# A hybrid two-layer trunk on one core: softmax sums divide a head's result, queries negated, operands moved by pads, residual squares added on VectorE

## The chip, the cores and the metric

The kernel runs on 1 core of one Trainium2 chip. The metric is the device time of one execution in microseconds (us). TensorE is written PE, its weight loads PEld, VectorE DVE, ScalarE ACT, GpSimd POOL, and SyncE, which issues the DMAs, SP.

## The reference, cut to what matters

Two layers work on 256 tokens of 1024 features. In each, a token mixer (layer 0: a state-space mixer called S5; layer 1: causal attention with 12 heads of 64 and a linear bias by distance, ALiBi) runs beside a 4-head attention into 256 memory tokens; both are concatenated and go through one output projection, and a SwiGLU FFN follows. With 256 tokens the block-sparse attention is one block, so layer 1 is plain causal attention.

```python
scores = jnp.einsum('bshd,bmhd->bhsm', qh, mem_k)        # qh is scaled by 64 ** -0.5
p = jax.nn.softmax(scores, axis=-1)
out = jnp.einsum('bhsm,bmhd->bshd', p, mem_v)
...
s_own = jnp.where(dist_own >= 0, s_own - slopes * dist_own, NEG_INF)
p = softmax(s_own);  out = p @ v_own
...
x = x + jnp.concatenate([tok, mem_out], axis=-1) @ w_out[i]
h = _rmsnorm(x, ffn_norm_g[i])
x = x + (jax.nn.silu(h @ w_gate[i]) * (h @ w_up[i])) @ w_down[i]
```

## The kernel before, in words

**Layout.** Activations lie transposed: features on the 128 partitions, the 256 tokens along the row. Every fp32 operand of the large products is split into a high and a low part in the format fp32r (`split`, `split_hi`, `split_lo`), and `mm3` makes one product of three matmuls: high by high, high by low, low by high. In a matmul one operand is loaded into PE and stays (PEld shows the load), the other streams by.

**Weights** come in chunks of 128x1024 by DMA into `raw`; ACT or POOL writes `whi`, DVE or POOL writes `wlo` (`split_hi`, `split_lo`; L140, L158). `rings` opens the three pools, `plan` sets the order of the chunks and the engines for each.

**Stages.** S5 mixer with four memory heads (`mixers0`), `w_out`, gate and up products (`ffn`), the down product, then for layer 1 attention with 4 memory heads and 12 causal ones (`mixers1`), which ends with its own output projection, gate and up again, and last `finale`, where the down product takes the tokens as output partitions and the weights as the streaming operand.

**Order.** `ORDER0` and `ORDER1` are lists of step names; each is emitted in that order, and the framework's scheduler may move instructions of different steps past each other on an engine. Each engine then works strictly in its own order. For head i the steps are `s` (scores), `x` (maximum and exponential), `n` (division by the sum), `t` (transposition of the weights p on PE), `h` (split of the transposed p into `ph` and `pl`), `p` (product with the values, bank `pv`) and `o` (result into the concatenated activations, `gl` or `mcat`). There is one PSUM bank of kind `pv`, and two of kind `tp`.

**Heads in pairs.** Two heads of 64 make one 128-row tile. In `h_values` the values (high part in columns 0 to 63, low part in 64 to 127) are the loaded operand, and the weights p stream by, 256 columns for a memory head's halves and 256 and 128 for a causal head's; so the result stands with head features on the partitions, the low part's result in partitions 64 to 127. `h_out` adds the two halves.

**Residuals.** `residual` adds a product to x on DVE, writes the next norm's input (`scaled`: high part on ACT, low part on DVE) and squares x on ACT; `square` then adds the squares of tiles 1 to 6 on POOL (L199). This is done 8 times after each of `w_out`, the first down product and layer 1's output projection.

Of the kernel before, what the change touches and what calls it, by code (L numbers as in the profile page):

```python
# [17 lines left out]
P = 128  # L18
D = 1024
KT = D // P  # L20
T = 256
# [10 lines left out]
MAGIC = 12582912.0  # L32
SLOPES = [float(np.float32(2.0 ** (-8.0 * (n + 1) / HEADS))) for n in range(HEADS)]
# [30 lines left out]
tm4 turn2 xh0 rot3 wo5 sh1 nh0 xh1 wp4 rot4 scan3 th0 turn3 nh1 y2 st4 hh0 sh2 sh3 rot5 ab5 y3 ph0 th1 xh2 wp5 scan4  # L64
turn4 st5 scan5 gelu1 tm5 hh1 turn5 y4 nh2 y5 th2 xh3 gelu2 gA ph1 nh3 oh0 th3 gB hh2 oh1 gC0 ph2 oh2 gC1 hh3 ph3
oh3 gC2 gC3
# [8 lines left out]
q0 rc a4 v0a v0b rr q1 mq0 mq1 s0 s1 x0 kp0 n0 x1 ve0 a5 t0 n1 h0 s2 x2 a6 qp0 t1 s3 x3 h1 p0 qe0 n2 kp1 ke0  # L75
o0 n3 p1 a7 t2 h2 s4 x4 qp2 p2 s5 t3 h3 o1 qp1 a8 n4 qe1 t4 ke1 p3 kp2 x5 s6 s7 x6 h4 qp3 p4 qe2 n5 o2 a9 t5
v1a ke2 qe3 x7 n6 v1b h5 ve1 p5 t6 s8 x8 n7 s9 o3 t7 a10 kp3 a11 x9 h6 h7 o4 p6 n8 t8 qp4 o5 o6 qe4 n9 a12 h8
ke3 a13 p7 s10 s11 x10 v2a p8 o7 t9 o8 h9 n10 a14 x11 kp4 p9 t10 h10 n11 v2b p10 o9 ke4 t11 h11 ve2 s12 s13
kp5 p11 x12 qp5 x13 n12 n13 qe5 o10 o11 t12 ke5 a15 s14 x14 s15 t13 x15 h12 p12 n14 o12 w0 h13 p13 t14 n15 t15
h14 h15 p14 o13 o14 w1 p15 o15 w2 r0 r1 r2 w3 w4 w5 w6 w7 r3 r4 r5 r6 r7  # L80
# [6 lines left out]
class Trunk:  # L87
# [9 lines left out]
    def rings(self, ctx, nm, raw, hi, lo, ahead):  # L97
# [3 lines left out]
        self.n_raw = raw  # L101

# [84 lines left out]
    def square(self, sums, x, k):  # L187

        nc = self.nc
        if k == 0:  # L190
            sums.append(self.tmp.tile([P, T], F32, tag="acc", name="acc"))
            nc.scalar.activation(out=sums[0], in_=x, func=AF.Square)
            return
        s = self.tmp.tile([P, T], F32, tag="sq", name="sq")
        nc.scalar.activation(out=s, in_=x, func=AF.Square)  # L195
        if k == KT - 1:
            sums.append(s)
        else:
            nc.gpsimd.tensor_add(out=sums[0], in0=sums[0], in1=s)  # L199
# [103 lines left out]

    class Head:
        pass

    def mem_heads(self, out):
        hs = []
        for pr in range(2):
            for e in range(2):  # L310
                h = self.Head()
                h.slope, h.q, h.k, h.e = None, self.mq[pr], self.mk[pr], e
                h.vt, h.hd, h.out = self.mv, 2 * pr + e, out[pr]
                hs.append(h)
        return hs

    def moba_heads(self, p, q, k, vt, out):
        hs = []
        for e in range(2):
            h = self.Head()  # L320
            h.slope, h.q, h.k, h.e = SLOPES[2 * p + e], q, k, e
            h.vt, h.hd, h.out = vt, (2 * p + e) % 4, out
            hs.append(h)
        return hs

    def h_scores(self, h):
# [5 lines left out]
        if h.slope is None:  # L332
            h.blocks = [(0, slice(0, T)), (1, slice(T, 2 * T))]
            h.order, h.n0 = [0, 2, 1, 3], 0
# [3 lines left out]
        else:  # L338
            h.blocks = [(0, slice(0, P)), (1, slice(P, P + T))]
            h.order, h.n0 = [0, 1, 2], P  # L340
# [3 lines left out]
    def h_exp(self, h):  # L344
        nc, v = self.nc, self.nc.vector
        nm = self.small.tile([P, 2], F32, tag="nm", name="nm")
        if h.slope is None:
            src = h.s
            v.tensor_reduce(nm, src.rearrange("p (a b) -> p a b", a=2), axis=AX.X, op=ALU.max, negate=True)
# [7 lines left out]
        h.sm = self.small.tile([P, 2], F32, tag="sm", name="sm")  # L357
        h.p = self.tmp.tile([P, 512], F32, tag="p", name="p")
        for i, c in h.blocks:
            nc.scalar.activation(out=h.p[:, c], in_=src[:, c], func=AF.Exp, bias=nm[:, i:i + 1],  # L360
                                 accum_out=h.sm[:, i:i + 1])

    def h_norm(self, h):
        nc, v = self.nc, self.nc.vector
        ri = self.small.tile([P, 2], F32, tag="ri", name="ri")
        v.reciprocal(ri, h.sm)
        for i, c in h.blocks:
            v.tensor_scalar_mul(h.p[:, c], h.p[:, c], ri[:, i:i + 1])  # L368

    def h_turn(self, h):  # L370
        h.tp = self.bank("tp")
        for i, c in enumerate(h.order):
            self.nc.tensor.transpose(h.tp[:, i * P:(i + 1) * P], h.p[:, c * P:(c + 1) * P], self.ident)

    def h_split(self, h):
        n = len(h.order) * P
# [5 lines left out]
    def h_values(self, h):  # L382
        mm = self.nc.tensor.matmul
        n = len(h.order) * P
        o = h.o = self.bank("pv")
# [6 lines left out]
    def h_out(self, h):  # L392
        nc, v = self.nc, self.nc.vector
        r = slice(64 * h.e, 64 * h.e + 64)
        if h.e == 0:
            self.ot = self.tmp.tile([P, T], F32, tag="otile", name="otile")
        t = self.tmp.tile([P, T], F32, tag="ot", name="ot")
        nc.scalar.activation(out=t[r], in_=h.o[64:128, 0:T], func=AF.Copy)
        v.tensor_add(out=self.ot[r], in0=h.o[0:64, 0:T], in1=t[r])  # L399
        if h.e == 1:  # L400
            self.split(*h.out, self.ot)

    def head_blocks(self, do, nm, at):

        for k, f in (("s", self.h_scores), ("x", self.h_exp), ("n", self.h_norm),
# [495 lines left out]
    def mixers1(self, pool, xs, sums, cat, order):  # L901
# [43 lines left out]
        def alibi(i):  # L945

            sb = pool.tile([P, 384], F32, tag="sb", name="sb", bufs=3)
            self.nc.gpsimd.tensor_scalar(sb, self.dist, -SLOPES[i - MEMH], 1.0, op0=ALU.mult, op1=ALU.mult)
# [201 lines left out]
    def run(self):  # L1150
# [176 lines left out]
```

## Time and profile before

| | |
|---|---|
| three runs | 651.79, 659.34 and 661.03 us, median 659.34 |
| profiled execution, its own time | 652.99 us |
| its span, first to last instruction | 651.2 us |
| PE, PEld busy | 619.1, 589.0 us |
| DVE, ACT, POOL busy | 461.0, 363.8, 112.3 us |
| granted PE clock, mean | 0.981 |

The profiled execution lies with the fastest of the three runs; 1.8 us of its time lie outside the span. PE's records overlap, since matmuls are pipelined: how fast it works is read from the distance between the starts of matmuls, not from their durations. The stages of the profiled execution, by the weights and tiles that its rows name: S5 mixer with memory heads to 137 us, `w_out` to 161, gate and up to 280, down to 345, attention to 440 (its projection's first chunks among it), the rest of the projection to 460, gate and up to 581, `finale` to the end.

### The profile page before, as it was taken

What the parts mean: (1) busy time and instruction counts of PE and PEld (TensorE: products, weight loads), DVE (VectorE), ACT (ScalarE), POOL (GpSimd) and SP (SyncE); (2) the same over time, 40 slices, a digit from 0 to 9 for tenths busy, and PEclk for the clock granted to TensorE, in tenths of its full rate; (3) what the DMA queues carried; (4) which work ended last, traced back from release to release, by engine and by line L of the source; (5) the groups of instructions that cost most, each with busy time, mean ns of one, the idle gap of its engine ahead of it and who ended that gap; (6) DMA issues with size and microseconds to landing.
All of it is one profiled execution on the core that took longest, in us unless ns stands there. A gap on an engine that the chain in (4) does not pass through costs nothing. (4 is left out here: it accounts for less than half of the span.)

```text
span 651.2 us, 12337 instructions
## 1 busy us (share of the span) xinstructions
PE 619.1 (95%) x4808; PEld 589.0 (90%) x4808; DVE 461.0 (71%) x835; ACT 363.8 (56%) x651; POOL 112.3 (17%) x94
## 2 busy tenths in 40 slices
PE   7998889899999999999999999989999999999995
PEld 6887678799999999999999899979899999998884
DVE  7979778779766666655546989968676666664444
ACT  7494836667555555544444767747455555553333
POOL 2435531212000000001147522215000000000001
PEclk9999989999999999999999999989799999999998
DMA  7463231636555555555545234326455555554511
GB/s 222 166 192 113 66 98 57 201 131 224 183 193 195 194 196 195 178 180 183 192 174 202 103 129 136 126 98 192 148 180 194 194 195 194 196 195 164 192 64 66
DMA packets 35578, 105.82 MB, mean 162 GB/s; under 512 B 4032, under 2 KB 9280, under 8 KB 35520
## 3 DMA queue, kind: packets, MB, share of 16 engines
q1 hardware_dynamic: 35520, 105.03, 48.0%
q8 instruction: 38, 0.62, 0.4%
q14 instruction: 20, 0.16, 0.1%
HBM read 102.40 MB, written 1.05 MB: 159 GB/s over the span
## 5 line engine op out<-in xcount | busy, mean ns | idle before, releaser
L140 ACT ACTIVATE whi<-raw 128x1024 fp32r<-128x1024 f32 (+2 forms) x176 | 183.3, 1043 | 156.9 <-PE mm L183 108.2
L158 DVE TENSOR_TENSOR wlo<-raw,whi 128x1024 fp32r<-128x1024 f32 (+1 forms) x157 | 191.2, 1219 | 54.3 <-PE mm L1108 28.3
L1046 DVE TENSOR_TENSOR gu<-mm,rr 128x512 f32<-128x512 f32 x44 | 30.4, 692 | 51.3 <-PE mm L184 50.7
L158 POOL TENSOR_TENSOR wlo<-raw,whi 128x1024 fp32r<-128x1024 f32 (+2 forms) x19 | 44.6, 2355 | 45.4 <-issue 13.8
L199 POOL TENSOR_TENSOR acc<-acc,sq 128x256 f32<-128x256 f32 x18 | 17.8, 989 | 194.3 <-ACT sq L195 187.3
L184 PE MATMUL mm<-hh,wlo 128*128 128x256 f32 x176 | 49.8, 283 | 0.0
L182 PE MATMUL mm<-hh,whi 128*128 128x256 f32 x176 | 49.8, 283 | 0.0
L183 PE MATMUL mm<-hl,whi 128*128 128x256 f32 x176 | 49.8, 283 | 0.0
L262 ACT ACTIVATE hh<-ev 128x256 fp32r<-128x256 f32 x44 | 18.2, 418 | 36.7 <-DVE ev L1038 36.7
L1135 POOL TENSOR_TENSOR o<-xt,gf 128x256 f32<-128x256 f32 (+1 forms) x3 | 2.8, 919 | 186.2 <-DVE xt L1129 183.5
L182 PEld LDWEIGHTS mm<-hh,whi 128*128 128x128 f32 x176 | 33.8, 192 | 0.0
L184 PEld LDWEIGHTS mm<-hh,wlo 128*128 128x128 f32 x176 | 33.8, 192 | 0.0
L183 PEld LDWEIGHTS mm<-hl,whi 128*128 128x128 f32 x176 | 33.8, 192 | 0.0
L263 DVE TENSOR_TENSOR hl<-ev,hh 128x256 fp32r<-128x256 f32 x44 | 18.7, 426 | 19.7 <-ACT hh L262 19.7
L183 PE MATMUL mm<-xg7l,whi 128*128 128x256 f32 x102 | 28.7, 281 | 1.6 <-DVE xg7l L258 1.6
L182 PE MATMUL mm<-xg0h,whi 128*128 128x256 f32 x102 | 30.0, 294 | 0.0
L183 PE MATMUL mm<-xg6l,whi 128*128 128x256 f32 x102 | 28.4, 279 | 0.5 <-DVE xg6l L258 0.5
L182 PE MATMUL mm<-xg7h,whi 128*128 128x256 f32 x102 | 28.3, 277 | 0.4 <-ACT xg7h L257 0.4
L183 PE MATMUL mm<-xg0l,whi 128*128 128x256 f32 x102 | 28.4, 278 | 0.0
L184 PE MATMUL mm<-xg0h,wlo 128*128 128x256 f32 x102 | 28.4, 278 | 0.0
L184 PE MATMUL mm<-xg7h,wlo 128*128 128x256 f32 x102 | 28.3, 278 | 0.0
L182 PE MATMUL mm<-xg1h,whi 128*128 128x256 f32 x102 | 28.3, 278 | 0.0
(428 smaller groups left out, 2213.0 us busy)
## 6 DMA issues: line engine op xcount, KB each, us to landing
raw<-in_w_gu SPq DMA_DIRECT2D x88, 512.0 KB, 4.0
raw<-in_w_down SPq DMA_DIRECT2D x30, 512.0 KB, 3.2
raw<-in_w_qkv SPq DMA_DIRECT2D x18, 512.0 KB, 3.2
raw<-in_w_out SPq DMA_DIRECT2D x16, 512.0 KB, 3.3
raw<-in_w_down SPq DMA_DIRECT2D x16, 448.0 KB, 3.2
raw<-in_w_u SPq DMA_DIRECT2D x5, 512.0 KB, 4.2
raw<-in_w_q SPq DMA_DIRECT2D x4, 512.0 KB, 3.5
wx<-wo SPq DMA_DIRECT2D x12, 128.0 KB, 2.4
```

The lines of the kernel that those rows point to most:

```text
L140: nc.scalar.activation(out=hi, in_=raw, func=AF.Copy)
L158: e.tensor_sub(out=lo, in0=raw, in1=f32(hi))
L182: mm(out, ah, bh, start=(first and i == 0), stop=False)
L183: mm(out, ah, bl, start=False, stop=False)
L184: mm(out, al, bh, start=False, stop=(last and i == n - 1))
L199: nc.gpsimd.tensor_add(out=sums[0], in0=sums[0], in1=s)
L262: self.nc.scalar.activation(out=h, in_=x, func=AF.Copy)
L263: self.nc.vector.tensor_sub(out=l, in0=x, in1=f32(h))
L1046: v.tensor_mul(t, ps, rr.rearrange("p a b -> p (a b)"))
L1135: (nc.gpsimd if i else v).tensor_mul(o[n][:, c], r, gf[:, a:b])
```

## The change

- **Division.** `h_norm` is gone, and with it the `n` steps in both lists. The exponential's sums of a pair of heads stay in one tile `sm` of four columns. `h_values` is turned round: a 128x128 block of `ph` or `pl` is the loaded operand, the 128 columns of values stream by, and the result stands with queries on the partitions; both heads of a pair write one `pv` bank. `h_out` does nothing for a pair's first head; for the second it takes the reciprocals, adds high and low parts, multiplies by the reciprocals, transposes the result back on PE in two 128x128 pieces, and splits it.
- **Sign.** The scaled row norm is written with -0.125, so scores come out negated; the bias is positive, the maximum becomes a minimum, and the exponential takes scale -1. The step that negated the maximum (L356) is gone.
- **Pads.** `shift` takes a small tile at the start of a pool, so that everything behind it stands further on in each partition.
- **Squares.** The sum of squares in `square` is added on DVE.

```diff
-            nc.gpsimd.tensor_add(out=sums[0], in0=sums[0], in1=s)
+            nc.vector.tensor_add(out=sums[0], in0=sums[0], in1=s)
...
+SHIFT_A, SHIFT_B, SHIFT_HID = 40, 16, 16
+    def shift(self, pool, n):
+        if n:
+            self.nc.vector.memset(pool.tile([P, n], F32, tag="pad", name="pad", bufs=1), 0.0)
...
-            nc.scalar.activation(out=r8, in_=ps[:, 0:T], func=AF.Copy, scale=0.125)
+            nc.scalar.activation(out=r8, in_=ps[:, 0:T], func=AF.Copy, scale=-0.125)
...
-            mx = self.small.tile([P, 2], F32, tag="mx", name="mx")
             for i, c in h.blocks:
-                v.tensor_tensor_reduce(out=src[:, c], in0=src[:, c], in1=h.s[:, c], scale=1.0, scalar=-3e38,
-                                       op0=ALU.add, op1=ALU.max, accum_out=mx[:, i:i + 1])
-            v.tensor_scalar_mul(nm, mx, -1.0)
+                v.tensor_tensor_reduce(out=src[:, c], in0=src[:, c], in1=h.s[:, c], scale=1.0, scalar=3e38,
+                                       op0=ALU.add, op1=ALU.min, accum_out=nm[:, i:i + 1])
...
-    def h_norm(self, h):
-        nc, v = self.nc, self.nc.vector
-        ri = self.small.tile([P, 2], F32, tag="ri", name="ri")
-        v.reciprocal(ri, h.sm)
-        for i, c in h.blocks:
-            v.tensor_scalar_mul(h.p[:, c], h.p[:, c], ri[:, i:i + 1])
...
-        w = [h.vt[:, k, h.hd].rearrange("p a b -> p (a b)") for k in range(2)]
-        mm(o[:, 0:T], w[0], h.ph[:, 0:T], start=True, stop=False)
-        mm(o[:, 0:T], w[0], h.pl[:, 0:T], start=False, stop=False)
-        mm(o[:, h.n0:T], w[1], h.ph[:, T:n], start=False, stop=False)
-        mm(o[:, h.n0:T], w[1], h.pl[:, T:n], start=False, stop=True)
+        if h.e == 0:
+            h.pair.o = self.bank("pv")
+        for i, parts in enumerate(h.parts):
+            o = h.pair.o[:, (2 * h.e + i) * P:(2 * h.e + i + 1) * P]
+            for k, c in enumerate(parts):
+                w = h.vt[:, k, h.hd].rearrange("p a b -> p (a b)")
+                for z in (h.ph, h.pl):
+                    self.nc.tensor.matmul(o, z[:, c * P:(c + 1) * P], w, start=(k == 0 and z is h.ph),
+                                          stop=(k == len(parts) - 1 and z is h.pl))
...
-        t = self.tmp.tile([P, T], F32, tag="ot", name="ot")
-        nc.scalar.activation(out=t[r], in_=h.o[64:128, 0:T], func=AF.Copy)
-        v.tensor_add(out=self.ot[r], in0=h.o[0:64, 0:T], in1=t[r])
-        if h.e == 1:
-            self.split(*h.out, self.ot)
+        v.reciprocal(ri, h.pair.sm)
+        nc.scalar.activation(out=t, in_=o[:, :, 1], func=AF.Copy)
+        v.tensor_add(out=t, in0=o[:, :, 0], in1=t)
+        v.tensor_mul(w.rearrange("p i e d -> p e i d"), t.rearrange("p (e i) d -> p e i d", e=2),
+                     ri.rearrange("p (e i) -> p e i", e=2)[:, :, :, None].to_broadcast([P, 2, 2, 64]))
+        tp = self.bank("tp")
+        for i in range(2):
+            nc.tensor.transpose(tp[:, i * P:(i + 1) * P], w[:, i].rearrange("p e d -> p (e d)"), self.ident)
+        self.split(*h.out, tp[:, 0:T])
...
+        self.shift(pool, SHIFT_HID)
-                self.rings(sy, "a", 4, 2, 2, 1)
+                self.rings(sy, "a", 4, 2, 2, 1, SHIFT_A)
-            self.rings(sx, "b", 5, 5, 4, 2)
+            self.rings(sx, "b", 5, 5, 4, 2, SHIFT_B)
```

In the built program, the byte address of the two operands of the fp32r products within their partition, modulo 256 (streaming operand, loaded operand), and the number of matmuls that have it:

| product | streaming x columns | before | after | matmuls |
|---|---|---|---|---|
| gate and up, `w_out`, q and k of layer 1 | x or `gl`, 256 | 160, 224 | 160, 224 | 2832 |
| down, layer 0 | `hh`, `hl`, 256 | 224, 224 | 32, 224 | 528 |
| `finale` | weights, 256 | 224, 224 | 224, 32 | 132 |
| `finale` | weights, 512 | 224, 224 | 224, 32 | 198 |
| S5 gate (`gA` to `gC`) | `yh`, `yl`, 256 | 160, 0 | 160, 96 | 108 |
| values of layer 1 (`v`) | weights, 256 | 224, 160 | 224, 160 | 144 |

The first pad of the second ring (`SHIFT_B`) leaves the weights where they were, since the small tiles in front of them take 64 bytes less.

How the change moves instructions. On PE, in the middle of layer 1's attention, at head 8 (`p8`): before, four matmuls with the values loaded, then the transposition of the next head's p (L373) and a product.

```order
L387 MATMUL pv<-ph,vt 128x256
L388 MATMUL pv<-pl,vt 128x256
L389 MATMUL pv<-ph,vt 128x128
L390 MATMUL pv<-pl,vt 128x128
L373 MATMUL tp<-con,p 128x128 x3
L182 MATMUL mm<-xg0h,whi 128x256
```

On PE at the same head after (L394 are the values, L413 the transposition back of the pair before, heads 6 and 7, L376 that of the next head's p).

```order
L394 MATMUL pv<-vt,ph 128x128
L394 MATMUL pv<-vt,pl 128x128
L394 MATMUL pv<-vt,ph 128x128
L394 MATMUL pv<-vt,pl 128x128
L394 MATMUL pv<-vt,ph 128x128
L394 MATMUL pv<-vt,pl 128x128
L413 MATMUL tp<-con,otile 128x128 x2
L376 MATMUL tp<-con,p 128x128 x3
```

Four matmuls have become six, and PE has a new instruction that waits for ACT and DVE.

On DVE in `w_out`, around the low parts `xg3l` and `xg4l` of the norm's input; before:

```order
L258 SCALAR_TENSOR_TENSOR xg3l<-xa_1518,par,xg3h 128x256
L1005 TENSOR_TENSOR xa_1519<-mm,xa_1519 128x256
L158 TENSOR_TENSOR wlo<-raw,whi 128x1024
L258 SCALAR_TENSOR_TENSOR xg4l<-xa_1519,par,xg4h 128x256
L1005 TENSOR_TENSOR xa_1519<-mm,xa_1519 128x256
```

On DVE at the same place after.

```order
L264 SCALAR_TENSOR_TENSOR xg3l<-xa_1524,par,xg3h 128x256
L205 TENSOR_TENSOR acc<-acc,sq 128x256
L1018 TENSOR_TENSOR xa_1525<-mm,xa_1525 128x256
L164 TENSOR_TENSOR wlo<-raw,whi 128x1024
L264 SCALAR_TENSOR_TENSOR xg4l<-xa_1525,par,xg4h 128x256
L205 TENSOR_TENSOR acc<-acc,sq 128x256
```

Each sum of squares stands behind the low part of its own tile, ahead of the next residual sum.

## Rows read from the trace of the kernel before

**Rows 1.** The page: span, and busy time, share and instructions of PE and DVE.
```profile
span 651.2 us, 12337 instructions
...
PE 619.1 (95%) x4808; PEld 589.0 (90%) x4808; DVE 461.0 (71%) x835; ACT 363.8 (56%) x651; POOL 112.3 (17%) x94
```

**Rows 2.** Windows by stage: length, busy time and instructions by engine, PE clock, DMA share, GB/s.
```profile
core 0: us, PE busy (x) PEld busy (x) DVE busy (x) ACT busy (x) POOL busy (x), PEclk, DMA share, GB/s
...
90.00:137.00 47.00, 42.99 (x326) 38.46 (x326) 37.11 (x65) 31.87 (x74) 8.37 (x5) 1.00 0.39 125
...
345.00:440.00 95.00, 90.88 (x742) 85.73 (x741) 82.06 (x212) 61.82 (x149) 32.07 (x24) 0.98 0.37 130
```

**Rows 3.** Timeline of PE, gate and up of layer 0: start, duration, instruction (24 matmuls apart).
```profile
249.93 0.28 PE L182 MATMUL mm<-xg0h,whi 128*128 128x256 f32 x1
...
252.65 0.28 PE L182 MATMUL mm<-xg0h,whi 128*128 128x256 f32 x1
```

**Rows 4.** The same, down product of layer 0 (24 matmuls apart).
```profile
299.99 0.28 PE L182 MATMUL mm<-hh,whi 128*128 128x256 f32 x1
...
302.87 0.28 PE L182 MATMUL mm<-hh,whi 128*128 128x256 f32 x1
```

**Rows 5.** The same, values of layer 1, weights streaming (45 matmuls apart).
```profile
347.64 0.28 PE L183 MATMUL mm<-wlo,xg0h 128*128 128x256 f32 x1
...
352.94 0.28 PE L183 MATMUL mm<-wlo,xg7h 128*128 128x256 f32 x1
```

**Rows 6.** The same, `finale`, one row of products apart: 9 matmuls of 512, 6 of 256.
```profile
599.76 0.40 PE L1107 MATMUL sc<-whi,hh 128*128 128x512 f32 x1
...
602.54 0.40 PE L1107 MATMUL sc<-whi,hh 128*128 128x512 f32 x1
```

**Rows 7.** Timeline of PE at head 15's values: weight loads and two matmuls.
```profile
436.29 0.19 PEld L389 LDWEIGHTS pv<-ph,vt 128*128 128x128 f32 x1
436.40 0.22 PE L389 MATMUL pv<-ph,vt 128*128 128x128 f32 x1
436.40 0.19 PEld L390 LDWEIGHTS pv<-pl,vt 128*128 128x128 f32 x1
436.46 0.28 PE L390 MATMUL pv<-pl,vt 128*128 128x128 f32 x1
436.51 0.19 PEld L182 LDWEIGHTS mm<-mcat,whi 128*128 128x128 f32 x1
```

**Rows 8.** Groups of DVE, 345 to 440 us: count, busy us, mean ns, idle before.
```profile
L368 DVE TENSOR_SCALAR p<-p,ri 128x256 f32<-128x256 f32 x20 | 14.9, 761 | 0.1
...
L399 DVE TENSOR_TENSOR otile<-pv,ot 64x256 f32<-64x256 f32 x16 | 6.6, 414 | 2.8 <-ACT ot L398 2.6
...
L368 DVE TENSOR_SCALAR p<-p,ri 128x128 f32<-128x128 f32 x12 | 4.3, 360 | 0.4
...
L356 DVE TENSOR_SCALAR nm<-mx 128x2 f32<-128x2 f32 x12 | 3.3, 271 | 0.0
```

**Rows 9.** A group of ACT, 345 to 440 us.
```profile
L398 ACT ACTIVATE ot<-pv 64x256 f32<-64x256 f32 x16 | 6.1, 380 | 4.8 <-PE pv L390 4.5
```

**Rows 10.** Waits of PE, 345 to 440 us: total, times, longest.
```profile
PE sc L341 <- DVE qqf L297: 2.8, 1, 2.8
```

**Rows 11.** Windows of 2 us behind that wait, columns as in rows 2.
```profile
424.00:426.00 2.00, 0.01 (x1) 0.00 (x0) 1.97 (x2) 1.36 (x2) 1.83 (x1) 1.00 0.50 188
...
428.00:430.00 2.00, 2.00 (x14) 1.86 (x13) 1.60 (x10) 0.43 (x2) 0.00 (x0) 0.56 0.87 348
430.00:432.00 2.00, 2.00 (x12) 2.00 (x12) 1.68 (x7) 1.88 (x9) 0.00 (x0) 0.59 0.00 0
```

**Rows 12.** Timeline of DVE and POOL in `w_out`.
```profile
153.56 0.74 POOL L199 TENSOR_TENSOR acc<-acc,sq 128x256 f32<-128x256 f32 x1 [2.81 <-ACT sq L195]
...
153.63 0.96 DVE L258 SCALAR_TENSOR_TENSOR xg4l<-xa,par,xg4h 128x256 fp32r<-128x256 f32 x1
...
160.68 0.47 DVE L258 SCALAR_TENSOR_TENSOR xg7l<-xa,par,xg7h 128x256 fp32r<-128x256 f32 x1
```

More of the change, by code (lines that the diff above doesn't have):

```diff
@@ L94, in pool, with rings @@
         return ctx.enter_context(self.tc.tile_pool(name=name, bufs=bufs, reuse_waits="tile", **k))
-    def rings(self, ctx, nm, raw, hi, lo, ahead):
+    def shift(self, pool, n):
+        if n:
+            self.nc.vector.memset(pool.tile([P, n], F32, tag="pad", name="pad", bufs=1), 0.0)
+    def rings(self, ctx, nm, raw, hi, lo, ahead, shift):
         self.ahead = ahead
@@ L309, in mem_heads @@
         for pr in range(2):
+            pair = self.Head()
             for e in range(2):
                 h = self.Head()
+                h.pair = pair
                 h.slope, h.q, h.k, h.e = None, self.mq[pr], self.mk[pr], e
@@ L318, in moba_heads @@
         hs = []
+        pair = self.Head()
         for e in range(2):
             h = self.Head()
+            h.pair = pair
             h.slope, h.q, h.k, h.e = SLOPES[2 * p + e], q, k, e
@@ L333, in h_scores @@
             h.blocks = [(0, slice(0, T)), (1, slice(T, 2 * T))]
-            h.order, h.n0 = [0, 2, 1, 3], 0
+            h.parts = [(0, 1), (2, 3)]
             for i, c in h.blocks:
@@ L339, in h_scores @@
             h.blocks = [(0, slice(0, P)), (1, slice(P, P + T))]
-            h.order, h.n0 = [0, 1, 2], P
+            h.parts = [(0,), (1, 2)]
             mm(s[:, 0:P], qf[r, 0:P], kf[r, 0:P], start=True, stop=True)
@@ L348, in h_exp @@
             src = h.s
-            v.tensor_reduce(nm, src.rearrange("p (a b) -> p a b", a=2), axis=AX.X, op=ALU.max, negate=True)
+            v.tensor_reduce(nm, src.rearrange("p (a b) -> p a b", a=2), axis=AX.X, op=ALU.min)
         else:
             src = h.sb
-            mx = self.small.tile([P, 2], F32, tag="mx", name="mx")
             for i, c in h.blocks:
-                v.tensor_tensor_reduce(out=src[:, c], in0=src[:, c], in1=h.s[:, c], scale=1.0, scalar=-3e38,
-                                       op0=ALU.add, op1=ALU.max, accum_out=mx[:, i:i + 1])
-            v.tensor_scalar_mul(nm, mx, -1.0)
-        h.sm = self.small.tile([P, 2], F32, tag="sm", name="sm")
+                v.tensor_tensor_reduce(out=src[:, c], in0=src[:, c], in1=h.s[:, c], scale=1.0, scalar=3e38,
+                                       op0=ALU.add, op1=ALU.min, accum_out=nm[:, i:i + 1])
+        if h.e == 0:
+            h.pair.sm = self.small.tile([P, 4], F32, tag="sm", name="sm")
         h.p = self.tmp.tile([P, 512], F32, tag="p", name="p")
         for i, c in h.blocks:
-            nc.scalar.activation(out=h.p[:, c], in_=src[:, c], func=AF.Exp, bias=nm[:, i:i + 1],
-                                 accum_out=h.sm[:, i:i + 1])
-    def h_norm(self, h):
-        nc, v = self.nc, self.nc.vector
-        ri = self.small.tile([P, 2], F32, tag="ri", name="ri")
-        v.reciprocal(ri, h.sm)
-        for i, c in h.blocks:
-            v.tensor_scalar_mul(h.p[:, c], h.p[:, c], ri[:, i:i + 1])
+            nc.scalar.activation(out=h.p[:, c], in_=src[:, c], func=AF.Exp, bias=nm[:, i:i + 1], scale=-1.0,
+                                 accum_out=h.pair.sm[:, 2 * h.e + i:2 * h.e + i + 1])
     def h_turn(self, h):
         h.tp = self.bank("tp")
-        for i, c in enumerate(h.order):
-            self.nc.tensor.transpose(h.tp[:, i * P:(i + 1) * P], h.p[:, c * P:(c + 1) * P], self.ident)
+        for c in range(h.parts[1][-1] + 1):
+            self.nc.tensor.transpose(h.tp[:, c * P:(c + 1) * P], h.p[:, c * P:(c + 1) * P], self.ident)
     def h_split(self, h):
-        n = len(h.order) * P
+        n = (h.parts[1][-1] + 1) * P
         h.ph = self.tmp.tile([P, 512], F32R, tag="ph", name="ph")
@@ L382, in h_values @@
     def h_values(self, h):
-        mm = self.nc.tensor.matmul
-        n = len(h.order) * P
-        o = h.o = self.bank("pv")
-        w = [h.vt[:, k, h.hd].rearrange("p a b -> p (a b)") for k in range(2)]
-        mm(o[:, 0:T], w[0], h.ph[:, 0:T], start=True, stop=False)
-        mm(o[:, 0:T], w[0], h.pl[:, 0:T], start=False, stop=False)
-        mm(o[:, h.n0:T], w[1], h.ph[:, T:n], start=False, stop=False)
-        mm(o[:, h.n0:T], w[1], h.pl[:, T:n], start=False, stop=True)
+        if h.e == 0:
+            h.pair.o = self.bank("pv")
@@ L393, in h_out @@
         nc, v = self.nc, self.nc.vector
[L394 to L401 removed]
+        ri = self.small.tile([P, 4], F32, tag="ri", name="ri")
@@ new lines, in h_out @@
+        v.reciprocal(ri, h.pair.sm)
+        o = h.pair.o.rearrange("p (a c d) -> p a c d", a=4, c=2)
+        t = self.tmp.tile([P, 4, 64], F32, tag="ot", name="ot")
+        nc.scalar.activation(out=t, in_=o[:, :, 1], func=AF.Copy)
+        v.tensor_add(out=t, in0=o[:, :, 0], in1=t)
+        w = self.tmp.tile([P, 2, 2, 64], F32, tag="otile", name="otile")
+        v.tensor_mul(w.rearrange("p i e d -> p e i d"), t.rearrange("p (e i) d -> p e i d", e=2),
+                     ri.rearrange("p (e i) -> p e i", e=2)[:, :, :, None].to_broadcast([P, 2, 2, 64]))
```

23 lines of the change are left out of this document (12 added, 11 removed).

## The prediction

> **What bounds the kernel now.** The page first: PE is busy in 95% of the span, DVE in 71% [rows 1]. PE is therefore the engine to count, but its share is an average over stages, so the windows by stage come next. In `w_out`, gate and up, down and `finale` the matmuls start back to back, and only the distance between their starts counts there: 24 matmuls take 2.72 us in gate and up, so 113.3 ns each [rows 3], 2.88 us in the down product, 120.0 ns [rows 4], and 45 take 5.30 us in layer 1's values, 117.8 ns [rows 5]; all stream 256 columns. In `finale` one row of products takes 2.78 us [rows 6]. In layer 1's attention PE is busy for 90.88 us of 95, DVE for 82.06; in the last part of layer 0's mixer PE for 42.99 of 47, DVE for 37.11 [rows 2]. In attention one wait is most of PE's idle time: 2.8 us for a DVE result [rows 10]. Behind it PE's granted clock is 0.56 and 0.59 of full for 4 us, the lower of its two levels (1.2 GHz), after a window in which PE did almost nothing [rows 11].
>
> I work against the profiled execution's 653.0 us. Three runs have the median 659.3; all four executions have the mean 656.3, so a sum against 653.0 goes up by 3.3 to be compared with a median of runs.
>
> **Pads.** The three distances above go with the operands' addresses modulo 256 (the table in the change): streaming less loaded address is -64 for gate and up (113.3 ns), 0 for down (120.0), +64 for layer 1's values (117.8). After the change down stands at 32 and 224, which is +64 modulo 256, and `finale` at 224 and 32, which is -64. I take the rows with the same difference. Down: 528 matmuls × (120.0 - 117.8) = -1.2 us; if -64 and +64 were alike it is 528 × 6.7 = -3.5, if the address doesn't matter 0. `finale`: 22 rows of 15 matmuls, × 6.7 ns = -2.2; 0 if addresses don't matter, and -3.5 if the excess grows with the 512-wide form, which I put at half as much again. The S5 gates move by 108 matmuls out of PE's tightest stretches: 0, or 108 × 5 ns = -0.5. Together -3.4 (0 to -7.5).
>
> A rule speaks against this term. The rows show excess starts that differ by stage, with the same form and back to back [rows 3 to 5]. The Trainium skill, "TensorE: Matmul & The Clock Gate", section "Step-by-step: what each phase is for", has it that PE reads the streaming operand and the loaded one through two independent ports, so that loading the next weights takes nothing from the running matmul. By that rule the pads would give nothing; the rows bear it out only so far as the 120.0 could belong to something else in that stage (rival D).
>
> **More instructions on PE.** A memory head's four matmuls of 256 columns become eight of 128, a causal head's four (two of 256, two of 128) become six, and each pair adds two transpositions back. Layer 1: 4 × 4 + 12 × 2 + 8 × 2 = 56; layer 0: 4 × 4 + 2 × 2 = 20. A shorter matmul doesn't pay in proportion, since each has its own load, and loads follow each other at 0.11 us (436.29, 436.40, 436.51) though the matmuls between have 128 columns [rows 7]. So 56 × 0.11 = +6.2 in attention, where PE is nearly full. In layer 0, 20 × 0.11 = 2.2 lie in a stretch with 4.0 us of idle PE; I take half, +1.1 (0 to 2.2). The floor for all is the idle time that they can fill, 4.1 us in attention [rows 2], so +2.1 there.
>
> By the same page of the Trainium skill, section "Back-to-back issue gap", a sustained stream of load and matmul takes 81 ns for 128 columns; 56 of them would be an estimated 4.5 us in place of 6.2. The 0.11 of the row decides.
>
> **Less work on DVE.** In attention the divisions go (14.9 + 4.3 us), the negated maxima (3.3) and one addition for each head (6.6) [rows 8]: 29.1. For each of 8 pairs come an addition and a multiplication, priced as the addition that goes, 0.414: 6.6. Net -22.5 of 82.06. The wait that this meets is PE's 2.8 us for `qqf`, where DVE was busy for 1.97 of 2 us [rows 10, 11]. I let all of it go, and with it the low clock behind, which costs 4 us × about 0.43 = 1.7. Of the other 1.3 us of idle PE (95 - 90.88 - 2.8) I let 0.4 go. That is -4.9 (0 if another transfer or ACT is late next, -5.8 at most). What is late next at that place is ACT's share of the same step, busy for 1.36 of those 2 us. In layer 0 the same edits, at layer 1's means, remove 4 × (2 × 0.761 + 0.414) = 7.7 and add 2 × 2 × 0.414 = 1.7, so -6.0 of DVE's 37.11; PE's idle time there is 4.0, of which I let 0.6 go (0 to 2.5).
>
> **A new wait on PE.** The back-transposition (L413) waits for a copy on ACT, 0.38 [rows 9], an addition and a multiplication on DVE, 0.41 each [rows 8]: 1.2 us after the pair's last value product. Behind it on PE stand the next head's transposition and all products; DVE, which is freed, waits for these. The program gives the cover: between a pair's last value product and its L413 the next head's matmuls stand, mostly 24 products, which is 2.7 us at 113.3 ns; behind the last pair 12, which is 1.4. So the cover is at least as long as the chain, if ACT and DVE take it up at once. I put +0.7, one of eight pairs with half of its chain uncovered; 0 if none, 8 × 1.2 = +9.7 if ACT and DVE are always busy with other work when the products end. The single `pv` bank is held by a pair until the addition is done, which is a part of the same chain and isn't counted twice.
>
> **Squares and sign.** One add of squares on POOL took 0.74 us, and DVE's low part at the same time 0.96, where the same operation without POOL took 0.47 [rows 12]. Moved to DVE, an add costs some 0.414 (the nearest DVE row, L399 [rows 8]) and the low part gets 0.49 back: -0.08 for each of 18 adds, -1.4 in all if each stood on the path. Since PE waits for few of them I take -0.3. The other bound: the add stands ahead of the next tile's residual sum, and where that is late, in the six adds behind layer 1's projection, 6 × 0.414 = +2.5. The sign costs nothing on ACT: the scale is a constant of an instruction that is there already.
>
> **Sum.** -3.4 + 6.2 + 1.1 - 4.9 - 0.6 + 0.7 - 0.3 = -1.2: 651.8 against the profiled execution, **655** as a median of runs. The two large terms, more instructions on PE and the returned wait, nearly cancel, and what is left is the pads.
>
> **The rivals.**
> - **B, the pads at full worth.** -64 and +64 behave alike and the 512-wide form gains more: -7.5 in place of -3.4, which gives 647.7, or 651 as a median. If the extra instructions in layer 0 are wholly hidden too (-1.1), the remaining idle time in attention goes (-0.9) and the squares pay in all places (-1.1), it is 644.6, or 648. For it: 113.3 is the only distance seen at a difference of 64 in the large products; against it: the 117.8 at +64.
> - **D, the pads do nothing.** The 120.0 belongs to another thing in the down product, such as weights that are being written into the ring while PE reads. Then 653.0 - 1.2 + 3.4 = 655.2, or 658.5. For it: one stage, one address, so the trace of before can't part the two. Against it: three stages with the same traffic of weights, three distances.
> - **C, the new wait is not covered**, and the kernel is slower. DVE is busy for 60 of 95 us in attention even then, and its order is fixed: if addition or multiplication stand behind a split of weights, PE stands at L413 for 1.2 us at each pair. 9.7 in place of 0.7, and the idle spells bring two more stretches of low clock like the one of [rows 11], 2 × 1.7: 651.8 + 9.0 + 3.4 = 664.2, or 667.5. It decides from a mean of 0.3 us at each L413 on, where the gain is used up. Against it: 24 products ahead of most of them, 2.7 us.
>
> **How the numbers follow.** A (the sum) 0.45, B 0.26, D 0.17, C 0.12. A, D and B without its extras lie between 650 and 660. A difference of 2%, about what a measurement of this kernel can tell from no change, is 13.2 us: below 646.2 only B's lower end reaches, with runs that scatter by 9 us: 0.11. Above 672.5 only C with more than two stretches of low clock: 0.04. Within 2%: 0.85. The range is 645 to 664: it takes in A, B and D with a scatter of some 4 us, and the milder half of C.
>
> **What would show it.** Starts of the down product: 117.8 ns (A), 113.3 (B), 120.0 (D). A row of `finale`: 2.68 us (A), less (B), 2.78 (D). Loads of the value products 0.11 us apart; if they are nearer to 0.08, my largest cost is too high. DVE's busy time in attention near 60 us, PE's wait of 2.8 us for `qqf` gone, and the clock behind it at 1.00. PE waits on L413 below 1 us in sum; 5 us or more is C. The low part `xg4l` at 0.47, with no add on POOL. I am wrong outside these if the scheduler's new order puts a stage's first weights later, or if stretches of low clock go or come elsewhere: one such stretch is 1.7 us, as large as most terms.

## The result: 0.6% slower, and the profile after

The changed kernel takes 660.33 us (median of 20 runs, 655.71 to 665.84), the kernel before 656.9 (20 runs, 650.46 to 664.58); the ratio is 1.0063, with a 95% interval of 1.0038 to 1.0087. Forecast was 655, a hair faster than before; the time lies in the stated range, but the sign was wrong. Runs of either kernel scatter by 10 to 14 us, and a part of why is found below. The ratios leave out the runs that lie more than 1.5% above the fastest of the same kernel, while the medians take in all, so the two can differ by up to 0.8% (in e1 to e4, where 9 of 21 runs of the kernel before are left out, and in e14, where 4 of its 10 are).

The page of the changed kernel, span and busy time, beside [rows 1]:

```profile
span 663.5 us, 12399 instructions
...
PE 631.9 (95%) x4884; PEld 602.5 (91%) x4884; DVE 439.6 (66%) x795; ACT 358.6 (54%) x641; POOL 94.6 (14%) x76
```

PE has the 76 more instructions (4884 against 4808), DVE 21 us less work. In the trace the stages were cut at the start of a product of each: for `w_out` its first one with a `gl` tile, for attention from layer 1's first value product to the last product of its projection, and `finale` to the last but one. All times in us:

| stage | before | after | after, again (e1) |
|---|---|---|---|
| S5 mixer and memory heads | 136.8 | 143.1 | 141.7 |
| `w_out` | 21.1 | 21.1 | 21.1 |
| gate and up, layer 0 | 121.9 | 125.6 | 125.6 |
| down, layer 0 | 67.58 | 66.38 | 66.38 |
| attention and projection | 106.8 | 109.7 | 109.6 |
| gate and up, layer 1 | 126.9 | 126.5 | 122.0 |
| `finale`, products | 62.74 | 62.99 | 63.00 |
| last product to the end | 7.3 | 8.0 | 7.9 |

The mixer's 6.3 us more (4.9 in e1) are not all the division's. The first scores of a memory head and the first `gl` product of `w_out`, before and then after:

```profile
92.51 0.38 PE L182 MATMUL sc<-mk0h,mqh 64*128 64x256 f32 x1
...
136.84 0.28 PE L182 MATMUL mm<-gl,whi 128*128 128x256 f32 x1
```

```profile
94.31 0.38 PE L188 MATMUL sc<-mk0h,mqh 64*128 64x256 f32 x1
...
143.06 0.28 PE L188 MATMUL mm<-gl,whi 128*128 128x256 f32 x1
```

After the change 1.8 us are lost before any head begins; the granted clock stayed at its lower level for 6.8 us from 83 us on, where it was 3.4 before, and 6.8 are also found with the old division (e3, e13 and others, with first scores at up to 95.5 us). From the first scores on it is 44.3 us before and 48.8 after (48.6 in e1), so 4.3 us more.

Waits of PE from 95 to 150 us, after (engine, what it waited for, total, times, longest):

```profile
PE tp L413 <- DVE otile L409: 3.6, 2, 3.1
```

This line is of the second profiled execution (e1); the first has 3.5 at the same place. Here is that wait in the first, at the last pair of memory heads, on PE, ACT and DVE:

```profile
132.33 0.28 PE L394 MATMUL pv<-mv,pl 128*128 128x128 f32 x1
...
134.53 0.28 PE L188 MATMUL mm<-yh,whi 128*128 128x256 f32 x1
137.88 0.60 PE L413 MATMUL tp<-con,otile 128*128 128x128 f32 x2 [3.07 <-DVE otile L409]
```

```profile
132.24 2.08 DVE L164 TENSOR_TENSOR wlo<-raw,whi 128x768 fp32r<-128x768 f32 x2
...
135.02 0.42 ACT L747 ACTIVATE gl<-ev 128x256 fp32r<-128x256 f32 x1 [0.95 <-DVE ev L745]
135.34 0.36 ACT L406 ACTIVATE ot<-pv 128x256 f32<-128x256 f32 x1
...
135.47 1.47 DVE L748 SCALAR_TENSOR_TENSOR gl<-ev,gl 128x256 fp32r<-128x256 f32 x1 [0.48 <-ACT gl L747]
136.86 0.41 DVE L407 TENSOR_TENSOR ot<-pv,ot 128x256 f32<-128x256 f32 x1
137.30 0.42 DVE L409 TENSOR_TENSOR otile<-ot,ri 128x256 f32<-128x256 f32 x1
```

The pair's last value product starts at 132.33, the transposition only at 137.88. ACT's copy of 0.36 us stands behind a gate's `gl`, which itself waited 0.95 us for DVE, and DVE had two splits of weights, 2.08 us, ahead of what it was to deliver; DVE's addition stands behind another `gl` of 1.47 us. PE has 13 products ahead of its transposition, which with a short wait for weights among them last to 134.8, and then stands for 3.07 us. What follows, in windows of 2 us (columns as in [rows 2]):

```profile
136.00:138.00 2.00, 0.12 (x1) 0.15 (x2) 1.97 (x4) 1.60 (x2) 0.65 (x1) 0.99 0.42 160
138.00:140.00 2.00, 2.00 (x11) 2.00 (x11) 1.29 (x2) 0.75 (x2) 0.00 (x0) 0.50 0.19 29
140.00:142.00 2.00, 2.00 (x13) 2.00 (x13) 0.85 (x2) 0.53 (x2) 0.00 (x0) 0.66 0.65 244
```

After a window in which PE worked for 0.12 us the granted clock is 0.50 and 0.66 in the mean, its lower level (1.2 GHz) for most of 4 us: an estimated 1.7 us more, at the price that the prediction takes from [rows 11].

The second surprise is gate and up of layer 0. Here and below, the distance is that between the starts of two matmuls that follow each other. Two matmuls 24 apart, after, beside [rows 3]:

```profile
249.80 0.28 PE L188 MATMUL mm<-xg7h,whi 128*128 128x256 f32 x1
...
252.63 0.28 PE L188 MATMUL mm<-xg7h,whi 128*128 128x256 f32 x1
```

That is 2.83 us, 117.9 ns each, where it was 113.3, though neither the instructions nor their addresses differ. In down, beside [rows 4], it is 2.83 us too, where it was 2.88:

```profile
299.74 0.28 PE L189 MATMUL mm<-hl,whi 128*128 128x256 f32 x1
...
302.57 0.28 PE L189 MATMUL mm<-hl,whi 128*128 128x256 f32 x1
```

### The profile page after: what moved, and what is told of

Same layout as the page of the kernel before. It is cut to its first block, busy times and chain, and to the rows that moved or that the text cites. A ratio compares the mean times of both kernels' runs of the same rounds, so it can differ in the third digit from the quotient of the medians.

```text
span 663.5 us, 12399 instructions
## 1 busy us (share of the span) xinstructions
PE 631.9 (95%) x4884; PEld 602.5 (91%) x4884; DVE 439.6 (66%) x795; ACT 358.6 (54%) x641; POOL 94.6 (14%) x76
## 5 line engine op out<-in xcount | busy, mean ns | idle before, releaser
L189 PE MATMUL mm<-xg1l,whi 128*128 128x256 f32 x102 | 28.6, 281 | 0.0
L190 PE MATMUL mm<-xg1h,wlo 128*128 128x256 f32 x102 | 28.6, 281 | 0.0
L188 PE MATMUL mm<-xg2h,whi 128*128 128x256 f32 x102 | 28.6, 281 | 0.0
```

The costliest lines, as they stand in the source:

```text
L188: mm(out, ah, bh, start=(first and i == 0), stop=False)
L189: mm(out, ah, bl, start=False, stop=False)
L190: mm(out, al, bh, start=False, stop=(last and i == n - 1))
```

## The experiments

Ratios are to the kernel before, on the same chip, with 95% intervals.

**e1, the changed kernel again.** No edit.

> The changed kernel once more, for a second profiled execution. Two theories on the distance between the starts of PE's 256-column matmuls, which in the first trace after the change was 117.8 ns in both gate and up stages, where it had been 113.3 before, though the addresses of their operands are the same. Theory 'start': a stretch of back-to-back matmuls falls into one of a few steady distances (113.3, 117.8, 120.0) by how it starts, and keeps it until PE is interrupted; then this execution may show 113.3 in one or both gate and up stages, and the time moves with it by about 1000 x 4.5 ns = 4.6 us a stage. Theory 'address': the distance is a property of the kernel's addresses or order; then 117.8 again in both stages. The wait on the back-transposition (L413) near 134 us, 3.1 us, with a stretch at the lower clock behind it, should be there again in either case. Ratio to the kernel before about 1.006.

660.27 us, 1.0090 (1.0054 to 1.0125; by the medians 1.003). Theory 'start' holds for layer 1, whose gate and up stage (24 matmuls apart) is shown first in the trace after, then in this one:

```profile
519.75 0.28 PE L189 MATMUL mm<-xg3l,whi 128*128 128x256 f32 x1
...
522.58 0.28 PE L189 MATMUL mm<-xg3l,whi 128*128 128x256 f32 x1
```

```profile
519.82 0.28 PE L188 MATMUL mm<-xg5h,whi 128*128 128x256 f32 x1
...
522.54 0.28 PE L188 MATMUL mm<-xg5h,whi 128*128 128x256 f32 x1
```

2.83 and 2.72 us: the same program, 117.9 and 113.3 ns. In this stage the distance belongs to the execution, not to the kernel, and is worth 4.5 us (126.5 and 122.0). In gate and up of layer 0 both executions have 117.7, so there the same isn't shown. Where the distance changes can be seen in the trace after, at 167 us:

```profile
166.63 0.28 PE L189 MATMUL mm<-xg7l,whi 128*128 128x256 f32 x1
166.75 0.28 PE L190 MATMUL mm<-xg7h,wlo 128*128 128x256 f32 x1
166.86 0.28 PE L227 MATMUL pv<-ones,acc 128*128 128x1 f32 x2
...
168.10 0.28 PE L188 MATMUL mm<-xg1h,whi 128*128 128x256 f32 x1
168.22 0.28 PE L189 MATMUL mm<-xg1l,whi 128*128 128x256 f32 x1
168.34 0.28 PE L190 MATMUL mm<-xg1h,wlo 128*128 128x256 f32 x1
168.46 0.28 PE L188 MATMUL mm<-xg2h,whi 128*128 128x256 f32 x1
```

Ahead of the eight small matmuls of the norm (L227) products are 0.11 to 0.12 us apart and, over `w_out` as a whole, 113.3 ns; behind them 117.8, and so for some 122 us up to the down product. In e4 it goes the other way at the same matmuls, from 117.8 to 113.4.

**e2, no pads.**

```diff
-SHIFT_A, SHIFT_B, SHIFT_HID = 40, 16, 16
+SHIFT_A, SHIFT_B, SHIFT_HID = 0, 0, 0
```

> The changed kernel with all three pads at 0. The address of the streaming operand less that of the loaded one is then 0 modulo 256 in nearly all fp32r products (3636 of 256 columns), gate and up included. Theory 'address': 120.0 ns in gate and up, w_out and down, a row of finale at 2.78 us; against 117.8 that is 2832 x 2.2 + 528 x 2.2 ns = 7.4 us, and finale 2.2, so +9.6 us on the changed kernel; against 113.3 in gate and up it would be +22. Theory 'start': the distances are those seen already, each stage drawn anew, no sign expected, within 5 us of the changed kernel.

673.25 us, 1.0304 (1.0248 to 1.0359), 13 us above the changed kernel. Gate and up:

```profile
249.83 0.28 PE L189 MATMUL mm<-xg6l,whi 128*128 128x256 f32 x1
...
252.71 0.28 PE L189 MATMUL mm<-xg6l,whi 128*128 128x256 f32 x1
```

2.88 us, 120.0 ns, and so in every long stretch. So both theories hold a part. Take the streaming operand's address less the loaded one's, modulo 256: at a difference of 0 the distance is fixed at 120.0, and at 192, which gate and up have otherwise, it is 113.3 or 117.8. The pads of the change mostly undo a harm of its own, since its smaller `small` tiles (64 bytes less) would have moved the weights onto the activations' address.

**e3, the pads alone on the kernel before.**

```diff
+        self.shift(pool, 16)          # hidden tiles
...
+        if nm == "a":
+            self.shift(self.raw, 24)
```

> The kernel before with the pads alone (the hidden tiles and the first ring; the second ring needs none, since the small tiles keep their size): down at 32 and 224, finale at 224 and 32, gates at 160 and 96. Theory 'address': down 117.8 ns in place of 120.0, a row of finale 2.68 us in place of 2.78, so -3.4 us, ratio 0.995, and gate and up at 113.3. Theory 'start': down leaves 120.0 only by chance; gate and up may be at 113.3 or 117.8; ratio 1.000 within the scatter.

657.23 us, 1.0034 (0.9986 to 1.0083): no gain that can be told, where 0.995 was expected. Down takes 66.59 us in place of 67.58, `finale` 62.99 in place of 62.74. The mean distance of `finale`'s 256-column matmuls falls from 118.9 to 115.6 ns, that of its 512-column ones rises from 229.4 to 232.9.

**e4, the back-transposition of layer 0's last pair later.** `h_out` cut in two, the chain on ACT and DVE (`lh3`) and transposition with split (`zh3`).

```diff
-st5 scan5 ... gC1 hh3 ph3 oh3 gC2 gC3
+st5 scan5 ... gC1 hh3 ph3 lh3 gC2 gC3 zh3
```

> The changed kernel with one step cut in two: for the last pair of memory heads of layer 0, the chain on ACT and DVE is issued where it was, and the back-transposition with its split is issued behind the last gate products (13 products ahead of it become 36, 2.7 us more cover). Theory 'wait': the 3.1 us at that transposition fall to below 1, the lower clock behind it goes (1.7 us), so -4 to -5 us on the changed kernel, ratio to the kernel before about 0.999. Rival 'matmuls': the change is slower by its 76 more instructions on PE, the wait only takes the place of another one in w_out (the result is its first operand), and the time stays within 1 us of the changed kernel.

660.61 us, 1.0111 (1.0039 to 1.0182): the time stays where the changed kernel's is, as the rival has it. The 3.1 us went to 0.5, the low clock behind it is gone, and the waits on these two lines are new:

```profile
PE mm L190 <- POOL wlo L164: 1.1, 1, 1.1
PE mm L188 <- ACT mcat L268: 0.9, 1, 0.9
```

The gate's low weights from POOL were late anyway, and the long wait had covered that; `w_out` begins with the very tile that the split writes. The mixer ends at 141.5, as in e1, but the first scores came 1.4 us later than there: from them on it is 46.9 us, against 48.6 in e1 and 44.3 before. So the later transposition gave back 1.7 of the 4.3 us, which is too little to be told in the time of six runs.

**e5 to e8, other differences.** The kernel before with pads of n words ahead of the second ring's weights and h words ahead of the hidden tiles: (16, 8), (40, 32), (8, 24), (24, 48).

> The kernel before with two other pads: streaming less loaded address, modulo 256, is 128 in gate and up, w_out, q and k (2856 matmuls of 256 columns), 32 in down, 224 in finale; so far 0 gave 120.0 ns in every stretch, 64 gave 117.8, 192 gave 113.3 in some stretches and 117.8 in others. Theory 'difference modulo 256': each difference has its own distances; 128 is farthest from 0 and gives 113.3 in all stretches. Theory 'modulo 128': 128 acts as 0 and gives 120.0, gate and up 2 x 1000 x 6.7 ns = 13 us longer than in the trace of before. Theory 'start': every difference but 0 gives 113.3 or 117.8 by the stretch. For 32 in down: between 113.3 and 120.0, the nearer to 120.0 the wider the reach of a conflict at 0.

> The kernel before with pads that make the difference 32 in gate and up, w_out, q and k, 128 in down and in finale. Theory 'difference modulo 256': down at 128 as gate and up in the run with 128 (113.3); gate and up at 32 as down in that run, the same distance for the same difference in another stage. Theory 'modulo 128': down 120.0. Theory 'start': 113.3 or 117.8 in each stretch, whatever the difference. Finale: a row of products 2.78 us at 0; its 512-column matmuls (231 ns at 0 and at 192) stay.

> The kernel before with pads that make the difference 160 in gate and up, w_out, q and k, 96 in down, 160 in finale. The S5 gates of the kernel before stand at 160 and start 118.5 ns apart, in short stretches. Theory 'difference modulo 256': gate and up 118 throughout, 9 us longer than the trace of before; down one distance. Theory 'start': 113.3 or 117.8 by the stretch in each, and the short stretches of the gates say nothing.

> The kernel before with pads that make the difference 96 in gate and up, w_out, q and k, 192 in down, 64 in finale. Theory 'difference modulo 256': gate and up as down in the run with 96; down as gate and up of the kernel before, 113.3 or 117.8; finale's row as with 192, 2.76 to 2.79 us. Theory 'start': no order in the differences other than 0.

Ratios 1.0109 (1.0075 to 1.0142), 1.0052 (1.0016 to 1.0087), 1.0074 (1.0036 to 1.0113) and 1.0117 (1.0048 to 1.0186). Mean distance of the 256-column products over whole stages, from all traces so far, by the difference of addresses modulo 256:

| difference | ns | seen in |
|---|---|---|
| 0 | 120.0 | down before; all stages of e2 |
| 32 | 116.7 to 117.7 | down e5; gate and up e6 |
| 64 | 117.8 | down after, e1, e3, e4 |
| 96 | 120.0 | down e7; gate and up e8 |
| 128 | 118.7 | gate and up e5; down e6 |
| 160 | 117.3 to 117.5 | gate and up e7 |
| 192 | 113.4 or 117.7 | gate and up before and after; down e8 113.4, down e11 117.8 |

The same difference gives the same distance in another stage, to within 1 ns or one of two values, so it is a matter of the difference, and of the seven seen only 192 reaches 113. Theory 'modulo 128' is refuted (128 isn't 120.0), and so is 'start' as it was put, since 96 and 128 have neither 113.3 nor 117.8; that 128 would give 113.3 was a miss too. Of the 512-column products of `finale`, those at 0 and 64 have 229 to 230 ns, the others 233 to 234.

**e9, the old division in layer 0 alone; e10, in layer 1 alone.** The changed kernel with the old `h_norm`, `h_turn`, `h_values`, `h_out` and order for one layer; the pads set so that the addresses stay.

> The changed kernel with the division and value products of the kernel before in layer 0 alone (its four memory heads with the steps n, and their order); layer 1, sign, pads (the same addresses) and squares as in the changed kernel. Theory 'layer 0': most of the loss is the two waits on the back-transposition there, 3.7 us, with the lower clock behind, 1.7 us, and some of 20 more instructions; S5 and memory heads end 4 to 6 us earlier, ratio to the kernel before 0.999 to 1.004. Rival 'layer 1': the loss is 56 more instructions on PE in attention; then this kernel stays near 1.006, and the time from the first value product of layer 1 to the end of its projection stays at 109.6 us in either case.

> The reverse: the changed kernel with the division and value products of the kernel before in layer 1 alone, layer 0, sign, pads (the same addresses) and squares as in the changed kernel. Theory 'layer 0': the time from the first value product of layer 1 to the end of its projection goes from 109.6 to 107 or 108 us, no more, since the new division gives back 4.9 of the 6.2 us that its instructions cost; the 3.1 us wait of layer 0 stays; ratio 1.003 to 1.008. Rival 'layer 1': 103.5 us or less, with the 56 instructions gone and DVE's wait not back, ratio at or below 1.000.

e9: 655.19 us, 0.9988 (0.9956 to 1.0019); the mixer ends at 137.8, attention takes 109.8. e10: 655.01 us, 0.9974 (0.9941 to 1.0007); the mixer ends at 144.0, attention takes **103.2** in place of 109.7. Each theory has its own number come true (e9's mixer, e10's ratio), so neither layer is the whole loss: either one gives back 0.7 to 0.9%. In e10 attention is 3.6 us shorter than before, with the old division in it, and PE's longest waits there are these:

```profile
PE sc L191 <- DVE qql L270: 0.9, 1, 0.9
PE pv L249 <- DVE diag L247: 0.4, 1, 0.4
```

The 2.8 us of [rows 10] are gone without the new division.

**e11, e12, the kernel before with one pad; and with the squares on DVE.** 48 words ahead of the hidden tiles.

```diff
+        self.shift(pool, 48)          # e11 and e12
...
-            nc.gpsimd.tensor_add(out=sums[0], in0=sums[0], in1=s)
+            nc.vector.tensor_add(out=sums[0], in0=sums[0], in1=s)   # e12
```

> The kernel before with one pad alone, 48 words at the head of the hidden tiles: the difference of addresses is 192 in down (in place of 0) and 64 in finale (0), everything else stays. From the distances by difference so far: down at 113.4 ns in place of 120.0 (-3.0 to -3.5 us), if it falls into that distance and not into 117.8 (-1.2); finale 62.53 us in place of 62.74. Ratio 0.994 to 0.998. If the distances are not a matter of the difference, no change.

> The same with the residual squares added on DVE, as in the change. By the prediction -0.3 us on that (bounds -1.4 and +2.5): the low part of the norm's input at 0.47 us in place of 0.96, PE's waits for the last low parts behind w_out and behind layer 1's projection (0.8 and 1.5 us in the trace of before) shorter. If the additions on DVE delay the residual sums instead, those waits are longer, and the ratio is up to 0.004 above that of the kernel without it.

e11: 656.76 us, 1.0017 (0.9985 to 1.0048), no gain where one was expected; down fell into 117.8 ns in its profiled execution, and `finale` takes 62.77 us, not 62.53. e12: 653.38 us, 0.9944 (0.9916 to 0.9973). Behind layer 1's projection the kernel before and e12 have these waits and windows (before first):

```profile
PE mm L183 <- DVE xg7l L258: 0.6, 1, 0.6
PE mm L183 <- DVE xg6l L258: 0.5, 1, 0.5
PE mm L182 <- ACT xg7h L257: 0.4, 1, 0.4
...
460.00:462.00 2.00, 2.00 (x11) 2.00 (x11) 1.63 (x5) 0.68 (x1) 0.00 (x0) 0.50 0.51 201
462.00:464.00 2.00, 2.00 (x11) 2.00 (x11) 1.22 (x8) 0.00 (x0) 0.00 (x0) 0.50 0.78 262
```

```profile
PE mm L187 <- DVE xg7l L262: 0.6, 1, 0.6
...
459.00:461.00 2.00, 2.00 (x20) 2.00 (x20) 2.00 (x5) 1.58 (x4) 0.00 (x0) 1.00 0.35 135
461.00:463.00 2.00, 1.39 (x11) 1.00 (x9) 1.41 (x2) 0.85 (x3) 0.00 (x0) 1.00 0.71 254
```

Before, three short waits followed each other and the clock fell for some 7 us; with the squares on DVE one is left and the clock stays. Gate and up of layer 1, at 113.3 ns in both, take 122.6 us in place of 126.9. The other traces agree: where all three waits stand (before, e3, e11, e13) the clock falls for 6.8 us, and where two, one or none are left (the other twelve, of which e5 to e8 have the squares on POOL) it doesn't.

**e13, the sign alone; e14, all but the division.** e13 is the kernel before with the sign's edits of the diff and 64 bytes in `small` that keep the addresses; e14 is e12 with the same.

> The kernel before with the sign alone: queries negated, minimum in place of maximum, no step that negates it; the small tiles are filled up so that every address is as before. Theory 'sign': the 12 instructions of 0.27 us that go from DVE are enough to end the wait of 2.8 us before head 12's scores, and the lower clock behind it goes; attention with its projection falls from 106.8 us to 103 to 104, ratio 0.994 to 0.997. Rival 'division': that wait needs the 22 us that the division takes from DVE; then attention stays at 106 to 107 us with the wait in it, ratio 0.998 to 1.000; the 103.15 us of the run with the old division in layer 1 would be due to the squares on DVE.

> All of the change but its division and value products, on the kernel before: sign, squares on DVE, and of the pads the one of 48 words at the hidden tiles. If the division is the whole loss: layer 0's mixer 137 to 138 us, attention with its projection 103 to 104, down 66.4 (or 64.5 if it falls into 113.3 ns), finale 62.8, the last low parts behind the projection without a stretch at the lower clock; about 9 us below the kernel before, ratio 0.985 to 0.992. If the parts share the same waits and don't add up: 0.994, as with pad and squares alone.

e13: 652.84 us, 0.9917 (0.9883 to 0.9951), a larger gain than the 0.994 expected at most; attention 102.9 us. The windows at the place of [rows 11] (head 12's scores):

```profile
428.00:430.00 2.00, 2.00 (x20) 1.79 (x18) 1.65 (x3) 1.18 (x2) 1.33 (x2) 1.00 0.17 33
430.00:432.00 2.00, 1.13 (x11) 0.67 (x9) 1.49 (x2) 1.34 (x4) 1.70 (x1) 1.00 0.59 229
432.00:434.00 2.00, 1.97 (x16) 1.84 (x17) 1.89 (x10) 1.05 (x5) 0.00 (x0) 1.00 0.46 135
```

No window in which PE does nothing, and the clock at 1.00. All eight traces without the sign's edits have the wait of 2.8 to 2.9 us and a stretch of low clock in attention, and all eight with them have neither. What the twelve instructions did by themselves isn't shown, though: with them gone the orders on PE, DVE and ACT are partly others, and DVE's work ahead of head 12 is quicker (`kkl` 1.07 us in e13, 2.01 before; one head's division 0.66 and 2.94).

e14: 650.94 us, **0.9856** (0.9812 to 0.9900), the lowest median of all kernels here; mixer 138.7, attention 102.9, down 66.4, `finale` 62.5. By the medians it is 5.9 us (0.9%) below the kernel before (656.82 here) and 1.4% below the changed kernel; by the ratios it would be 1.4% and 2.1%.

## Why the prediction was wrong, point by point

**The step that failed: the new wait on PE.** The prediction put +0.7 us on L413, "one of eight pairs", and so counted layer 1's pairs alone; layer 0's two had no term. And it took the chain as 1.2 us, its three instructions, "if ACT and DVE take it up at once". At the last pair of layer 0 both were in the middle of splits of weights and gates: 5.5 us from the last value product to the transposition, 2.5 us of it covered by products, 3.1 us of standing, and an estimated 1.7 us at the lower clock behind. From the first scores to `w_out` it is 48.8 and 48.6 us in the two traces of the changed kernel (50.2 in e2, 49.7 in e10, with a longer stretch at the lower clock), and 44.3 in ten of the eleven traces with the old division there (45.7 in e8): +4.3, where the sum had +1.1 and -0.6. The 20 more instructions are the small part: from the first scores to the last value product it is 38.0 us after and 37.7 before.

It was rival C's mechanism, at a place that C didn't name. In layer 1, where C looked for it, PE waits 0.2 us on L413 in sum: the cover there was as estimated. In both layers it is 3.7 us, between the below 1 of the sum and the 5 of C. e4 shows that the wait isn't all of the 4.3: without it the gates' late weights and the late split took a part of its place, and only taking the division back (e9) gave all of it back.

**The wait that was to come back was credited to the wrong edit.** Attention was forecast at +2.0 us (6.2 - 4.9 + 0.7) and came to +2.9, nearly right by luck: one of its two large terms belongs to another edit. The 56 more instructions are sized well: e10 against after is 103.2 against 109.7, 6.5 us for 6.2, and the value products start 0.11 us apart, as [rows 7] had it. Some 0.9 of the 6.5 are not instructions: in the four traces with the new division in layer 1 and a difference of 192 (after, e1, e4, e9) the projection's products are 117.2 to 117.5 ns apart, in the seven with the old one 113.5 to 114.0, and those of v, q and k a little farther too; why isn't shown. But the 2.8 us and the clock behind went with the sign's edits, which take nothing away but 12 instructions of 0.27 us on DVE (e13: -3.8 us, forecast -4.9 for both together). The division took some 17 us of DVE's time in attention (e10 against after), and PE's waits on the steps of the heads add up to 1.1 us with it as without. So it has costs alone: 6.5 us in layer 1 and 4.3 in layer 0. e14 has everything else, with one pad in place of three, and the lowest median.

**Pads.** Down: -1.2 us, as the sum had it to the tenth (67.58 to 66.38); with the pads it left 120.0 ns in both kernels (after, e3), so D is refuted there. `finale`: +0.25 in place of -2.2, the mis-sized term: the gain of 132 matmuls of 256 columns was there, 3.3 ns each, but the 198 of 512 columns, which I had priced like them, lost 3.4 ns. What follows the last product is 0.6 us longer in the traces with a pad ahead of the second ring (7.8 to 8.0 us) than in those without (7.3 to 7.4); what does it wasn't looked into.

The Trainium skill, "TensorE: Matmul & The Clock Gate", section "Step-by-step: what each phase is for", by whose rule of two independent read ports the pads would give nothing, spoke for rival D. The measurement decides against it as a rule for this stream: e2 differs from the changed kernel in pads alone and is 13 us slower, and its matmuls are at 120.0 ns in every stage. That it is a conflict of the two reads is not shown; shown is that the difference of the two addresses sets the distance.

**Squares.** -0.3 was too small: about -4.3 us (e12 against the kernel before in layer 1's gate and up), of which 0.9 are two of the waits and the rest the clock behind them. The prediction priced the additions; the waits that they feed, and the clock after those, weren't in the term.

**The sum.** -0.9 (pads), +0.6 (the end), +4.3 (layer 0), +2.9 (attention), -4.3 (squares) is +2.6 us; measured are +4.1 (2.5 to 5.7). What is left is smaller than the draw of a gate and up stage, 4.5 us. Two misses of about 4 us, the wait in layer 0 and the squares, have opposite signs and cancel, so that the time lies in the range is in part luck.

## What to carry to other kernels

A chain that crosses engines and ends in front of PE costs its length in their queues, not the sum of its instructions: for each place where it stands, read what ACT and DVE are in the middle of, in every stage and not in the largest alone. A wait that an edit is to remove may go with a far cheaper one: try the cheap edit alone first, and see what is left for the dear one. Two traces of a kernel can differ before the changed part begins, so count from the last point that the change can't have reached. An edit that changes a tile's size moves the addresses of all that lies behind it, so keep the addresses fixed while the edit is tried.

## What the runs showed of the hardware

- A stream of fp32r matmuls of 256 columns, each with its own load, starts every 113.3 to 120.0 ns by the difference of its operands' addresses modulo 256: 120.0 at 0 and at 96, and 113.3 at 192 alone of the seven multiples of 32 seen (0 to 192).
- At 192 the stream has two steady distances, 113.3 and 117.8 ns. The same program shows either (e1 and after, layer 1), and a stretch keeps its own until something comes between (the eight small matmuls of the norm, at 166.9 us). What draws it stays open. At 4.5 us a stage it can be a part of the scatter of the runs; only the profiled executions were read for it.
- A wait costs more than itself when the clock falls behind it: after 3.07 us of waiting it was at its lower level for 3.4 us, and after three waits of 1.5 us together (before, e3, e11, e13) for 6.8 us, which costs more than the waits.
